# Two-layer hybrid block on one core: large SBUF tiles moved to multiples of 1024 bytes, and VectorE shuffles for a DRAM round trip in the delta rule

## The chip, the cores and the metric

The kernel runs on one core of a Trainium2 chip. The metric is device time in microseconds (us) of one execution; three executions of the kernel before took 1622.04, 1630.62 and 1631.97 us, so the median is 1630.62 us.

## The reference

Two layers, each a half-step SwiGLU, a mixer, and another half-step SwiGLU, over 256 tokens of width 1024:

```
for l in range(DEPTH):                      # DEPTH = 2
    x = x + 0.5 * swiglu(rms_norm(x, ffn1_norm[l]), ...)
    x = x + hybrid_mixer(rms_norm(x, mix_norm[l]), w_in[l], ...)
    x = x + 0.5 * swiglu(rms_norm(x, ffn2_norm[l]), ...)
```

The mixer projects to 11,536 columns and has three branches: a gated linear recurrence (A), dilated windowed attention with 12 heads (B), and a gated delta rule with 8 heads in chunks of 64 tokens (C). Each branch is projected, gated and summed. For each head and chunk the delta rule solves a unit lower triangular system:

```
a = where(strict, einsum('bhnid,bhnjd->bhnij', kb, kc) * decay, 0)
sol = triangular_solve(a + eye(64), concat([vb, kb * exp(gam)]), lower=True, unit_diagonal=True)
```

## The kernel before

**Main matmuls.** Activations are kept transposed (features on partitions, 256 tokens in the free dimension). Each float32 operand of a projection is split into a rounded part and a remainder, both in the type fp32r: tiles `wh` and `wl` for weights, and two slots `s` of 256 columns (1024 bytes per partition) for activations. Each 128x128 weight block then takes three matmuls (high by high, high by low, low by high). In `stationary` (line 479) the weights are the stationary operand, a slice of 128 columns (512 bytes) of `wh` or `wl`, and a slot is the moving operand (256 columns). In `moving` (line 506), used only for the attention's q, k and v projections, the roles are swapped: a 128-column half of a slot is stationary, and 256 columns of `wh` or `wl` move. The results go to PSUM tiles `big`.

**Weights.** SyncE's queue loads 512 KB groups into one of six `raw` tiles, ScalarE (sometimes VectorE) rounds 1024 columns into `wh`, and VectorE subtracts to get `wl` (`convert`, line 430). 24 matmuls use one such chunk.

**Order.** All instructions are recorded by a planner at build time. It keeps a modelled clock for each engine, adds a cost to it for every instruction (`_cost`, line 327), and runs small tasks (Python generators) between main matmuls when their inputs should be there by those clocks. TensorE executes the recorded order as it stands, so a small matmul that stands too early holds back the main ones behind it. `until` lets the planner's TensorE clock run on, with no main matmul recorded, while the next main matmul's input is not due.

**Delta rule.** `pair` (line 994) handles two heads, eight times in all (four in each layer). It cuts 16x16 diagonal blocks out of the triangular matrix into `A16` (128 partitions x 64 columns). The substitution inside a block needs each row on all 16 partitions of that block. So `A16` is written to DRAM (`rd`, 32 KB) and read back into `RR` with every row repeated on 16 partitions (512 KB), both through SyncE's queue, on which the weight loads are issued too; the planner's task clock is moved on by 5.5 and then 8.5 us. GpSimd then does 15 steps of a multiply and a subtraction each (lines 1136 to 1140). TensorE joins the blocks (the 32x32, 64x64 and 128x128 matmuls into PSUM tiles `sm`), and the result `yc` feeds branch C. Attention (`heads4`) runs alongside and gives `yb` to branch B.

**Places in SBUF.** The pool places tiles one after another. In the built program, before the change, `raw`, `wh`, `wl`, `X`, `zr` and `ssq` start 960 bytes past a multiple of 1024 (the first `raw` at byte 26,560, the first `wh` at 51,136), because `cst` (2070 columns) and `prm` (440 columns) come first. The two small tiles `eps_n` and `half` stand behind `ssq` and happen to fill the 64 bytes that are missing, so `tiny`, `arena` and the slots start at multiples of 1024 (102,400, 106,496 and 163,840). A stationary slice of `wh` or `wl` therefore starts 448 or 960 bytes past a multiple of 1024, and the slot that moves against it at a multiple of 1024. In `moving` it is the other way round: the stationary half slot starts at a multiple of 512, and the moving slice at 960.

Of the kernel before, what the change touches and what calls it, by code (L numbers as in the profile page):

```python
# [10 lines left out]
F32 = mybir.dt.float32  # L11
# [6 lines left out]
P = 128  # L18
L = 2
# [20 lines left out]
KEEP, KEEP2 = 3072, 2048  # L40
ARENA_COLS = 14336
NSLOT = 60
SPARE = 4
SLACK = (800.0, 1500.0, 1500.0, 1500.0, 1500.0, 600.0)
URGENT = 2
# [54 lines left out]
def flat_chunks():  # L100
    return [c for layer in all_jobs() for jobs in layer for job in jobs for c in job[2]]


def group_chunks(chunks):
    groups, cur, cols = [], [], 0
    for c in chunks:
        w = c[3] * c[5]
        if cur and cols + w > GROUP_COLS:
            groups.append((cur, cols))
            cur, cols = [], 0  # L110
        cur.append(c)
        cols += w
    groups.append((cur, cols))
    return groups
# [60 lines left out]
class Arena:  # L175
    def __init__(self, pr, ap, unit):
        self.pr, self.ap, self.unit = pr, ap, unit
        self.n = ap.shape[1] // unit
        self.busy = [False] * self.n
        self.stamp = [0.0] * self.n  # L180
        self.peak = 0
# [123 lines left out]
def _free(ap):  # L305
    n = 1
    for x in ap.shape[1:]:
        n *= x
    return n


class Engine:
# [16 lines left out]
    def _cost(self, name, a, k):  # L329
        key = self._key  # L330
        if key == "pe":
            lhsT = k["lhsT"] if name == "matmul" else a[1]
            rhs = k["rhs"] if name == "matmul" else a[2]
            n, m = _free(rhs), _free(lhsT)
            if lhsT.dtype == F32R:
                return max(0.46 * n, 0.83 * m)
            if name == "transpose":
                return 0.84 * max(n, m)
            if m <= 32 and lhsT.shape[0] <= 32:
                return 40.0  # L340
            if m <= 64 and lhsT.shape[0] <= 64 and n <= 64:
                return 100.0
            return 1.7 * max(n, m)
        n = _free(a[0])
        if name == "tensor_reduce":
            n = _free(a[1])
        if key == "a":
            c = 93 + 0.833 * n
            for x in ("scale", "bias", "accum_out"):
                c += 93 * (not isinstance(k.get(x, 0.0), float) and x in k)  # L350
            func = a[2] if name == "activation" else None
            sets = TABLES.get(func)
            if sets and self._pr.table not in sets:
                self._pr.table = sets[0]
                c += 1283
            return c
        if key == "g":
            return (330 + 160 * n) if k.get("op") == ALU.pow else 350 + 0.6 * n
        if name == "reciprocal":
            return 68 + 6.3 * n  # L360
        fast = name in ("tensor_copy", "tensor_scalar") and a[1].space != PSUM
        c = 68 + (0.52 if fast else 1.04) * n
        if name in ("scalar_tensor_tensor", "tensor_scalar") and not isinstance(a[2], float):
            c += 60
        if k.get("accum_out") is not None:
            c += 60
        return c
# [5 lines left out]
class Prog:  # L373
    def __init__(self, ctx, tc, io):
        self.tc, self.nc, self.io = tc, tc.nc, io
        nc = self.nc
        self.clock = {"pe": 0.0, "v": 0.0, "a": 0.0, "g": 0.0}
        self.table = None
        self.cur = self.main = Task(None, 0.0, 0)
        self.step, self.used = set(), {}  # L380
        self.tasks = []
        self.pe, self.v = Engine(self, "pe", nc.tensor), Engine(self, "v", nc.vector)
        self.a, self.g = Engine(self, "a", nc.scalar), Engine(self, "g", nc.gpsimd)
        sb = ctx.enter_context(tc.tile_pool(name="sb", bufs=1))
        ps = ctx.enter_context(tc.tile_pool(name="ps", bufs=1, space=PSUM))
        dr = ctx.enter_context(tc.tile_pool(name="dr", bufs=1, space=bass.MemoryType.DRAM))
        self.cst = sb.tile([P, CST["_n"]], F32, name="cst")
        self.prm = sb.tile([P, L * PRM["_n"]], F32, name="prm")
        self.raw = [sb.tile([P, GROUP_COLS], F32, name=f"raw{i}") for i in range(NRAW)]
        self.wh = [sb.tile([P, 1024], F32R, name=f"wh{i}") for i in range(NCONV)]  # L390
        self.wl = [sb.tile([P, 1024], F32R, name=f"wl{i}") for i in range(NCONV)]
        self.X = sb.tile([P, KD, T], F32, name="X")
        self.zr = sb.tile([P, T], F32, name="zr")
        self.ssq = sb.tile([P, T], F32, name="ssq")
        self.eps_n = sb.tile([P, 1], F32, name="eps_n")
        self.half = sb.tile([P, 8], F32, name="half")
        self.tiny_t = sb.tile([P, 1024], F32, name="tiny")
        self.ar_t = sb.tile([P, ARENA_COLS], F32, name="arena")
        self.tiny = Arena(self, self.tiny_t, 8)
        self.slots = Slots(self, sb, NSLOT)  # L400
        self.ar = Arena(self, self.ar_t, 64)
        self.big = Banks(self, [ps.tile([P, 512], F32, name=f"big{i}") for i in range(NBIG)])
        self.sm = Banks(self, [ps.tile([P, 512], F32, name=f"sm{i}") for i in range(8 - NBIG)])
        self.gdram = [dr.tile([16, P], F32, name=f"gd{l}") for l in range(L)]
        self.rdram = [[dr.tile([P, 64], F32, name=f"rd{l}_{i}") for i in range(4)] for l in range(L)]
        self.rc = [self.tiny.get(16).ap for _ in range(L)]
        self.ea = [self.tiny.get(8) for _ in range(L)]
        self.qg = [self.tiny.get(6) for _ in range(L)]
        self.groups = group_chunks(flat_chunks())
        self.chunk_at = []  # L410
        off = 0
        self.goff = []
        for gi, (cs, cols) in enumerate(self.groups):
            self.goff.append(off)
            c0 = 0
            for c in cs:
                self.chunk_at.append((c, gi, c0, c[3] * c[5]))
                c0 += c[3] * c[5]
            off += P * cols
        self.unread = [len(cs) for cs, _ in self.groups]  # L420
        self.cursor = 0
        self.dma_next = 0
        self.dma_clock = 0.0
        self.raw_t = {}
        self.conv_t = {}
        self.conv_next = 0
        self.when = {}
        self.ops = {}
        self.prepared = set()
        self.nsq = None  # L430
        self.npair = 4
# [111 lines left out]
    def get(self, cols):  # L543
        b = None
        if cols == T:
            b = self.slots.get(F32, SPARE)
        return b or self.ar.get(cols, self.keep())
# [480 lines left out]
    def pair(self, l, h0):  # L1028
# [6 lines left out]
        src = self.gdram[l].rearrange("(t h) i -> h t i", t=2)  # L1035
# [30 lines left out]
        ssk, ssq, c, cn, rb = self.tinies(5, 4)  # L1066
        bt = self.beta.v("p (t h) -> p h t", t=2)[:, h0:h0 + 2, :]
        c4 = lambda x: x.v("p (h t) -> p h t", h=2)
        for hh, h in enumerate(heads):
# [8 lines left out]
            n = 2 * hh  # L1078
# [36 lines left out]
        t1, A16, RR = yield from self.spaces([128, 64, 1024])  # L1115
# [4 lines left out]
        a16 = A16.v("p (n j) -> p n j", n=4)  # L1120
        self.v.tensor_tensor(a16, t4[:, :, 0, :], t4[:, :, 1, :], op=ALU.add)
        yield
        self.nc.sync.dma_start(self.rdram[l][h0 // 2], A16.ap)
        self.cur.t += 5500.0
        yield
        src = self.rdram[l][h0 // 2].rearrange("(b k) c -> b (k c)", k=16)
        self.nc.sync.dma_start(RR.ap, src.unsqueeze(1).to_broadcast([8, 16, 1024]))
        t1.free()
        A16.free()
        self.cur.t += 8500.0  # L1130
        yield
        r4 = RR.v("p (k n j) -> p n k j", n=4, k=16)
        M16, tmp = yield from self.spaces([64, 64])
        m16 = M16.v("p (n j) -> p n j", n=4)
# [21 lines left out]
        b = yield from self.bank()  # L1156
# [9 lines left out]
        b = yield from self.bank()  # L1166
# [13 lines left out]
        b = yield from self.bank()  # L1180
# [19 lines left out]
        b = yield from self.bank()  # L1200
# [16 lines left out]
        b = yield from self.bank()  # L1217
# [9 lines left out]
        b = yield from self.bank()  # L1227
# [27 lines left out]
        b = yield from self.bank()  # L1255
# [7 lines left out]
        b = yield from self.bank()  # L1263
# [8 lines left out]
        for hh in range(2):  # L1272
            n = 2 * hh + 1
# [3 lines left out]
        b = yield from self.bank()  # L1277
# [38 lines left out]
        b = yield from self.bank()  # L1316
# [388 lines left out]
```

## Time and profile before

| what | value |
|---|---|
| median of three executions | 1630.62 us (1622.04 to 1631.97) |
| profiled execution | 1627.63 us, span 1625.4 us |
| mean granted TensorE clock | 0.994 |
| busy in the span: TensorE | 1602.4 us (99%) |
| VectorE, ScalarE, GpSimd | 1159.2 (71%), 936.7 (58%), 139.3 us (9%) |
| DMA queue of the loads, share of 16 engines | 53.7% |

TensorE is called busy wherever a matmul is in flight. One main matmul is in flight for about 280 ns and the next starts some 115 ns after it, so a share of 99% doesn't tell how fast they follow each other: that is read from the distance between starts. The layers run from about 6 to 822 us and from 822 to 1622 us; the first SwiGLU of a layer takes some 190 us, the mixer 435, the second SwiGLU 187.

### The profile page before, as it was taken

To read this page: it belongs to the slowest core of one execution; us is meant where nothing else is said; L and a number is where in the kernel's file an instruction comes from. 1 tells how busy PE (TensorE), PEld (TensorE's weight loads), DVE (VectorE), ACT (ScalarE), POOL (GpSimd) and SP (SyncE) were. 2 spreads that over 40 slices of the span, in tenths; PEclk is the share of its full clock that TensorE was granted. 3 is DMA by queue.
4 is the path that set the end of the run, shared out by engine and by line. 5 is a ranking of instruction groups with operands and counts; after the bars stand their busy time and mean duration, and the time that the engine had idled before them with its cause. 6 is when DMAs were issued, how large, how long until landed. Compare 5 with 4: busy or idle time off the path is not lost. (4 is left out here: it accounts for less than half of the span.)

```text
span 1625.4 us, 34428 instructions
## 1 busy us (share of the span) xinstructions
PE 1602.4 (99%) x13952; PEld 1560.0 (96%) x13952; DVE 1159.2 (71%) x2172; ACT 936.7 (58%) x1643; POOL 139.3 (9%) x280
## 2 busy tenths in 40 slices
PE   9999999999999999999999999999999999999999
PEld 8999999989988999999999999999898899999999
DVE  8666588987973667666566656989878756676653
ACT  7544456878854546444454445568887555554442
POOL 0000000345002000000000000003540120000000
PEclk9999999999998999999999999999999999999999
DMA  8655656544343565555555555656443345655562
GB/s 304 186 187 179 193 179 194 164 162 133 120 129 107 163 204 184 187 188 178 188 192 183 182 185 185 195 176 182 139 140 122 123 131 189 190 184 185 181 188 86
DMA packets 84942, 279.04 MB, mean 172 GB/s; under 512 B 10256, under 2 KB 15664, under 8 KB 84784
## 3 DMA queue, kind: packets, MB, share of 16 engines
q1 hardware_dynamic: 84784, 276.85, 53.7%
q8 instruction: 109, 1.79, 0.4%
q14 instruction: 49, 0.40, 0.1%
HBM read 275.49 MB, written 1.33 MB: 170 GB/s over the span
## 5 line engine op out<-in xcount | busy, mean ns | idle before, releaser
L323 PE MATMUL big<-s,wh 128*128 128x256 f32 (+1 forms) x7520 | 1346.3, 281 | 7.0 <-DVE s L323 6.0
L323 PEld LDWEIGHTS big<-s,wh 128*128 128x128 f32 (+1 forms) x7520 | 1151.0, 188 | 17.4 <-DVE s L323 6.8
L323 PE MATMUL big<-s,wl 128*128 128x256 f32 (+1 forms) x3760 | 1053.6, 280 | 0.0
L323 DVE TENSOR_TENSOR wl<-raw,wh 128x1024 fp32r<-128x1024 f32 (+3 forms) x523 | 620.8, 1187 | 248.4 <-ACT wh L323 245.2
L323 ACT ACTIVATE wh<-raw 128x1024 fp32r<-128x1024 f32 (+4 forms) x497 | 509.1, 1025 | 361.8 <-PE big L323 168.8
L323 PEld LDWEIGHTS big<-s,wl 128*128 128x128 f32 (+1 forms) x3760 | 705.3, 188 | 2.8 <-issue 1.8
L323 ACT ACTIVATE s<-s 128x256 fp32r<-128x256 f32 (+1 forms) x213 | 85.2, 413 | 116.6 <-DVE s L323 116.0
L323 POOL TENSOR_TENSOR tiny<-tiny,half 128x4 f32<-128x4 f32 (+1 forms) x28 | 38.6, 1378 | 1102.0 <-DVE tiny L323 1083.9
L323 PE MATMUL sm<-arena 128*128 128x128 f32 (+7 forms) x1440 | 114.0, 238 | 9.7 <-DVE arena L323 6.9
L323 PEld LDWEIGHTS sm<-arena 32*32 32x32 f32 (+5 forms) x1440 | 85.8, 138 | 30.2 <-issue 9.3
L323 PE MATMUL big<-wh,s 128*128 128x256 f32 x576 | 110.2, 287 | 0.0
L323 POOL TENSOR_TENSOR arena<-arena 128x60 f32<-128x60 f32 (+14 forms) x240 | 98.6, 411 | 62.6 <-DMA arena<-rd 44.7
L323 DVE TENSOR_TENSOR s<-s,s 128x256 fp32r<-128x256 f32 (+1 forms) x181 | 75.7, 422 | 36.5 <-ACT s L323 36.1
L323 PEld LDWEIGHTS big<-wh,s 128*128 128x128 f32 x576 | 89.6, 189 | 1.2
L323 DVE SCALAR_TENSOR_TENSOR s<-big,prm,s 128x255 f32<-128x255 f32 (+2 forms) x183 | 85.6, 477 | 6.6 <-ACT s L323 5.3
L323 DVE TENSOR_TENSOR arena<-big,zr 128x512 f32<-128x512 f32 x88 | 60.9, 692 | 34.8 <-PE big L323 34.5
L323 PE MATMUL big<-wl,s 128*128 128x256 f32 x288 | 82.1, 285 | 0.0
L323 ACT ACT_TABLE_LOAD x63 | 80.8, 1283 | 1.7 <-PEq L1697 0.7
L323 ACT ACTIVATE arena<-sm 128x128 f32<-128x128 f32 (+6 forms) x152 | 48.8, 323 | 37.6 <-PE sm L323 35.1
L323 ACT ACTIVATE s<-big 128x256 f32<-128x256 f32 x53 | 20.2, 382 | 62.1 <-PE big L323 62.1
L323 PEld LDWEIGHTS big<-wl,s 128*128 128x128 f32 x288 | 54.5, 189 | 0.4
L323 ACT ACTIVATE s<-big,prm 128x256 f32<-128x256 f32 x53 | 26.5, 499 | 45.2 <-PE big L323 45.0
(110 smaller groups left out, 772.3 us busy)
## 6 DMA issues: line engine op xcount, KB each, us to landing
raw<-wts SPq DMA_DIRECT2D x435, 512.0 KB, 3.7
raw<-wts SPq DMA_DIRECT2D x64, 448.0 KB, 3.6
raw<-wts SPq DMA_DIRECT2D x16, 384.0 KB, 3.1
arena<-rd SPq DMA_DIRECT2D x8, 512.0 KB
arena<-rgw SPq DMA_DIRECT2D x4, 512.0 KB, 5.2
arena<-gd SPq DMA_DIRECT2D x16, 128.0 KB, 4.7
X<-x SPq DMA_DIRECT2D x4, 256.0 KB, 4.9
raw<-wts SPq DMA_DIRECT2D x4, 256.0 KB, 3.2
```

The source lines that it names most:

```text
L323: r = f(*a, **k)
```

## The change

Three edits. The tiles `eps_n` and `half` move ahead of `raw`, and an unused tile of 252 columns follows them. In the built program `raw`, `wh`, `wl`, `X`, `zr` and `ssq` now start at multiples of 1024 bytes (the first `raw` at 27,648, the first `wh` at 52,224), and `tiny`, `arena` and the slots still do (103,424, 107,520, 164,864). The planner's cost of a main matmul goes from 0.46 to 0.445 ns a column (from 117.8 to 113.9 ns for 256 columns). In `pair`, the write to `rd` and the read back into `RR` are replaced by 15 VectorE shuffles: the shuffle for row k copies, inside each group of 32 partitions, partition 16*(c//16)+k to partition c, for 64 columns, into columns 64k to 64k+63 of `RR`.

```diff
+PAD = 252
...
-                return max(0.46 * n, 0.83 * m)
+                return max(0.445 * n, 0.83 * m)
...
+        self.eps_n = sb.tile([P, 1], F32, name="eps_n")
+        self.half = sb.tile([P, 8], F32, name="half")
+        sb.tile([P, PAD], F32, name="pad")
         self.raw = [sb.tile([P, GROUP_COLS], F32, name=f"raw{i}") for i in range(NRAW)]
...
-        self.eps_n = sb.tile([P, 1], F32, name="eps_n")
-        self.half = sb.tile([P, 8], F32, name="half")
...
-        self.rdram = [[dr.tile([P, 64], F32, name=f"rd{l}_{i}") for i in range(4)] for l in range(L)]
...
-        self.nc.sync.dma_start(self.rdram[l][h0 // 2], A16.ap)
-        self.cur.t += 5500.0
-        yield
-        src = self.rdram[l][h0 // 2].rearrange("(b k) c -> b (k c)", k=16)
-        self.nc.sync.dma_start(RR.ap, src.unsqueeze(1).to_broadcast([8, 16, 1024]))
         t1.free()
+        for k in range(1, 16):
+            self.v.stream_shuffle(RR[:, k * 64:k * 64 + 64], A16.ap, [16 * (c // 16) + k for c in range(32)])
+            if k % 5 == 0:
+                yield
         A16.free()
-        self.cur.t += 8500.0
-        yield
```

Since costs and tasks change, the planner records another order. On VectorE, in the first layer's mixer where the first pair cuts out `A16` (the row `arena<-arena 128x64`), the change has the shuffles in groups of five between the convolutions (`s<-big,prm,s`) and the weights' subtractions (`wl<-raw,wh`):

```order
L324 TENSOR_TENSOR arena<-arena,cst 128x128
L324 SCALAR_TENSOR_TENSOR s_3526<-big_91,prm,s_3526 128x253
L324 TENSOR_TENSOR arena<-arena 128x64
L324 SCALAR_TENSOR_TENSOR s_3563<-big_92,prm,s_3563 128x255
L324 STREAM_SHUFFLE arena<-arena 128x64 x5
L324 TENSOR_TENSOR s_3345<-s_3345,s_2725 128x256
L324 SCALAR_TENSOR_TENSOR s_3563<-big_92,prm,s_3563 128x254
L324 TENSOR_TENSOR wl_83<-raw_75,wh_78 128x1024
L324 SCALAR_TENSOR_TENSOR s_3563<-big_92,prm,s_3563 128x253
L324 STREAM_SHUFFLE arena<-arena 128x64 x5
L324 CAST wh_79<-raw_70 128x1024
...
L324 STREAM_SHUFFLE arena<-arena 128x64 x5
```

All fifteen stand within nine rows of VectorE's order. On SyncE's queue the same place before had the two transfers among the weight loads (`raw<-wts`); the second waits there until the first has landed:

```order
L598 DMA raw_69<-wts 128x1024
L1123 DMA rd_0_100<-arena 128x64
L598 DMA raw_70<-wts 128x1024
L1127 DMA arena<-rd_0_100 128x1x1024
L598 DMA raw_71<-wts 128x1024
```

In the change only weight loads stand there, and the sixteen rows of `rd` are gone from SyncE's order. On TensorE, the first matmuls of branch B's projection in the first layer (tile `big_91`) are followed before by the longest row of small matmuls in the program, 92 of them with no main matmul between; these are its first and last rows, and the main matmul that follows (`s_6190` is branch B's input):

```order
L323 MATMUL big_91<-s_5700,wl_80 128x256
L323 MATMUL sm_93<-arena 128x128
L323 MATMUL sm_93<-arena 128x256
L323 MATMUL sm_96<-arena 128x128
L323 MATMUL sm_96<-arena 128x256
L323 MATMUL sm_95<-arena 32x16 x16
...
L323 MATMUL sm_93<-cst,arena 128x128
L323 MATMUL sm_96<-cst,s_5193 128x128
L323 MATMUL big_91<-s_6190,wh_75 128x256
```

In the change no row of small matmuls in the first layer is longer than 21; the longest is now at the same place of the second layer, with 54:

```order
L324 MATMUL big_91<-s_14986,wl_82 128x256
L324 MATMUL sm_96<-arena 32x32 x12
L324 MATMUL sm_97<-arena 64x64 x4
L324 MATMUL sm_94<-s_15444,s_15406 64x64 x4
...
L324 MATMUL sm_96<-arena 128x128 x2
L324 MATMUL sm_94<-arena 128x128 x2
L324 MATMUL big_91<-s_15495,wh_77 128x256
```

So the place where the planner ran out of main matmuls moved from the first layer to the second and became shorter. In all, 167 groups of small matmuls stand among the main ones before, and 165 in the change.

## Rows read from the trace of the kernel before

**Rows 1.** The page: the span, and each engine's busy time, share of the span and instructions.

```profile
span 1625.4 us, 34428 instructions
PE 1602.4 (99%) x13952; PEld 1560.0 (96%) x13952; DVE 1159.2 (71%) x2172; ACT 936.7 (58%) x1643; POOL 139.3 (9%) x280
```

**Rows 2.** The page's costliest groups, those of the main matmuls: how many, busy time, mean ns of one, and idle time before them. `s,wh` is a slot moving against weights, `wh,s` weights moving against half a slot.

```profile
L323 PE MATMUL big<-s,wh 128*128 128x256 f32 (+1 forms) x7520 | 1346.3, 281 | 7.0 <-DVE s L323 6.0
L323 PE MATMUL big<-s,wl 128*128 128x256 f32 (+1 forms) x3760 | 1053.6, 280 | 0.0
L323 PE MATMUL big<-wh,s 128*128 128x256 f32 x576 | 110.2, 287 | 0.0
L323 PE MATMUL big<-wl,s 128*128 128x256 f32 x288 | 82.1, 285 | 0.0
```

**Rows 3.** TensorE's busy time and number of matmuls in four windows of 50 us in which only main matmuls run, the granted clock, the DMA engines' share and GB/s.

```profile
50.00:100.00 50.00, 50.00 (x427) 1.00 0.61 188
560.00:610.00 50.00, 50.00 (x444) 1.00 0.61 198
700.00:750.00 50.00, 50.00 (x427) 1.00 0.56 179
1360.00:1410.00 50.00, 50.00 (x427) 1.00 0.62 191
```

**Rows 4.** TensorE's timeline where the first projection of the form `moving` begins: start, length of the group, and how many matmuls are in it.

```profile
324.87 0.28 PE L323 MATMUL big<-wh,s 128*128 128x256 f32 x1
324.99 0.28 PE L323 MATMUL big<-wl,s 128*128 128x256 f32 x1
...
325.33 0.28 PE L323 MATMUL big<-wl,s 128*128 128x256 f32 x1
...
326.35 0.28 PE L323 MATMUL big<-wl,s 128*128 128x256 f32 x1
```

**Rows 5.** The same view inside two longer pieces of the form `moving`: 24 matmuls from the first row to the second, 39 from the third to the fourth.

```profile
358.11 0.28 PE L323 MATMUL big<-wl,s 128*128 128x256 f32 x1
...
360.93 0.28 PE L323 MATMUL big<-wl,s 128*128 128x256 f32 x1
...
395.32 0.28 PE L323 MATMUL big<-wl,s 128*128 128x256 f32 x1
...
399.74 0.28 PE L323 MATMUL big<-wl,s 128*128 128x256 f32 x1
```

**Rows 6.** The same view of the form `stationary` around four small transposes.

```profile
539.01 0.28 PE L323 MATMUL big<-s,wl 128*128 128x256 f32 x1
...
539.71 0.28 PE L323 MATMUL big<-s,wl 128*128 128x256 f32 x1
...
539.95 0.60 PE L323 MATMUL sm<-cst,arena 128*128 128x128 f32 x4
...
540.51 0.28 PE L323 MATMUL big<-s,wl 128*128 128x256 f32 x1
...
541.19 0.28 PE L323 MATMUL big<-s,wl 128*128 128x256 f32 x1
```

**Rows 7.** TensorE's busy time, number of matmuls and granted clock in the stretch of the 92 small matmuls (the windows' columns as in rows 3).

```profile
505.00:510.00 5.00, 3.92 (x47) 1.00 0.57 191
510.00:515.00 5.00, 2.93 (x84) 0.55 0.26 79
515.00:520.00 5.00, 4.82 (x45) 0.50 0.01 3
520.00:525.00 5.00, 5.00 (x29) 0.59 0.00 0
```

**Rows 8.** Groups of VectorE instructions, by shape: how many, busy time, mean ns of one, and idle time before them.

```profile
L323 DVE STREAM_TRANSPOSE arena<-arena 128x128 f32<-128x128 f32 x16 | 4.9, 306 | 0.2
L323 DVE TENSOR_TENSOR tiny<-tiny 128x8 f32<-128x8 f32 x28 | 4.6, 169 | 0.5 <-POOL tiny L323 0.4
L323 DVE TENSOR_TENSOR wl<-raw,wh 128x1024 fp32r<-128x1024 f32 x433 | 529.9, 1224 | 196.5 <-ACT wh L323 193.4
```

**Rows 9.** Busy time (and instructions) of PE, PEld, DVE, ACT and POOL in a stretch of a SwiGLU and in those parts of both mixers where the delta rule is prepared, then the granted clock, DMA share and GB/s.

```profile
50.00:100.00 50.00, 50.00 (x427) 50.00 (x427) 34.78 (x45) 23.96 (x36) 0.00 (x0) 1.00 0.61 188
198.00:325.00 127.00, 126.83 (x1040) 123.76 (x1039) 111.90 (x258) 88.33 (x142) 12.71 (x31) 1.00 0.56 180
325.00:405.00 80.00, 76.62 (x867) 71.85 (x866) 65.00 (x186) 63.21 (x157) 41.53 (x74) 0.98 0.47 150
405.00:440.00 35.00, 33.78 (x294) 31.30 (x294) 32.88 (x76) 29.34 (x67) 1.29 (x1) 1.00 0.29 92
1009.00:1133.00 124.00, 123.83 (x1014) 120.97 (x1014) 110.11 (x255) 86.65 (x141) 15.09 (x33) 1.00 0.59 182
```

**Rows 10.** SyncE's timeline at the first pair's round trip: start, length, the write to `rd` and the read back.

```profile
298.31 0.39 SPq L1123 DMA_DIRECT2D rd<-arena  x1
...
302.11 0.70 SPq L1127 DMA_DIRECT2D arena<-rd  x1
```

**Rows 11.** GpSimd's timeline at the same pair: its first run of substitution steps, with the idle time ahead and what ended it.

```profile
311.50 10.82 POOL L323 TENSOR_TENSOR arena<-arena 128x60 f32<-128x60 f32 x24 [13.14 <-DMA arena<-rd]
```

**Rows 12.** The page's form view of GpSimd: the first substitution step of all eight pairs (two instructions each), mean ns of one, and the idle time ahead of them.

```profile
L323 POOL TENSOR_TENSOR arena<-arena 128x60 f32<-128x60 f32 x16 | 6.8, 425 | 45.6 <-DMA arena<-rd 44.7
```

## The prediction

> **What bounds the kernel now.** I read the page's busy times first: TensorE is busy for 1602.4 of 1625.4 us, VectorE for 71% of the span, the others less [rows 1]. So all waits of TensorE together are 23 us, and a change that takes more than that must make TensorE's own work shorter. The work is 7520 + 3760 + 576 + 288 = 12,144 main matmuls [rows 2], each in flight for about 281 ns. That is not what one costs. They overlap, and the cost is the distance from one start to the next.
>
> For that I went to windows in which nothing but main matmuls runs. 50 us hold 427 of them in three windows and 444 in the fourth, all at a granted clock of 1.00, the upper level of 2.4 GHz [rows 3]. A window also counts the matmuls in flight at its edge, 2.4 on average (281 ns over some 118). So the distance is 50/424.6 = 117.8 ns in three windows and 50/441.6 = 113.2 ns in the fourth. TensorE has two paces at the same clock. Load doesn't separate them: the DMA share is 0.61 in a slow window and 0.61 in the fast one.
>
> The timeline shows where it changes pace. At the first projection of the form `moving` two matmuls start 0.12 us apart, and from 325.33 to 326.35 nine take 1.02 us, 113.3 ns each [rows 4]. The pace then holds: 24 matmuls in 2.82 us (117.5 ns) in one piece, 39 in 4.42 us (113.3 ns) in another [rows 5]. In the form `stationary`, six starts take 0.70 us before four small transposes and 0.68 us after them [rows 6], and the fast pace stays until 635 us. I went through all starts of main matmuls that follow each other. 10,479 distances are slow (116 to 123 ns, mean 117.8) and 1285 fast (112 to 115, mean 113.4); the rest are waits. By form the shares differ: in `moving` 419 of 742 are fast, in `stationary` 866 of 11,022, and 820 of these lie in the one stretch from 540 to 635 us.
>
> What differs between the forms is where operands start. In `moving` the stationary operand (half a slot) starts at a multiple of 512 bytes and the moving one 64 bytes below a multiple of 1024; in `stationary` it is the stationary one that is 64 below. I read this as: a stationary operand on a multiple of 512 lets TensorE fall into the fast pace, 1 to 4 matmuls after an interruption, while one that is 64 bytes off nearly always holds it in the slow one. It isn't the whole story. The stretch from 540 us is fast with the operand 64 off, and one piece in [rows 5] is slow with it aligned. The pace has two self-holding states, and the address shifts the odds.
>
> **Edit 1, the places.** After it all main matmuls have a stationary operand on a multiple of 512 and a moving one on a multiple of 1024. This pair of offsets does not occur among the main matmuls of before, so the trace can't show it. Bounds: no gain, or all 10,479 slow distances at 113.4, 10,479 x 4.4 ns = 46.1 us. I choose within by stage. The SwiGLUs and the tail of the second mixer hold 7038 slow distances (from 15 to 198, 635 to 1009 and 1345 to 1622 us) with hardly an interruption; I take all as fast, 7038 x 4.4 = 31.0 us. The other 3441 lie between the groups of small matmuls. After each of these some slow ones come first, so I take the share of `moving`, 56%: 3441 x 0.56 x 4.4 = 8.5 us. Sum 39.5 us. The faster pace asks for a chunk of weights every 2.7 us instead of 2.8. In the SwiGLU VectorE is busy 34.8 of 50 us, ScalarE 24.0 and the DMA engines 0.61 [rows 9], so all go up by 4% of that, and none becomes the bound.
>
> Against this stands a rule. The Trainium skill, page "SBUF — State Buffer", section "Who interferes with whom", says that TensorE and ScalarE never wait on anyone for SBUF, and the page "TensorE: Matmul & The Clock Gate", section "Back-to-back issue gap", gives N/2.4 + 2.5 ns with no address in it, an estimate of 109.2 ns for 256 columns. By these pages this edit would do nothing. The trace fits neither fully, since it has two paces, both above that estimate; the first rival below is the case in which addresses don't count.
>
> **Edit 2, the planner's cost.** 113.9 ns instead of 117.8 costs nothing itself. It moves small matmuls by as much as main ones get faster, if edit 1 works; if not, the planner's clock runs 3% ahead of TensorE, so other engines have more time, not less.
>
> **Edit 3, shuffles for the round trip.** 8 x 15 = 120 shuffles of 64 columns. The trace has none. The nearest rows are the transpose of 128 columns at 306 ns and an operation on 8 columns at 169 [rows 8]. On the line between them 64 columns are 169 + 137 x 56/120 = 233 ns (bounds 169 and 306). That is 28.0 us on VectorE (20.3 to 36.7), 14 in each mixer, 3.5 for a pair. It takes the place of 13.2 us from the write's issue at 298.31 to the first substitution step at 311.50 [rows 10, 11]. But of this GpSimd alone knew: its waits for the read back sum to 44.7 us [rows 12], and TensorE was filled with main matmuls meanwhile, so the shorter chain is worth nothing by itself. What hides the 14 us is VectorE's idle time: from 198 to 405 us it is busy 111.9 + 65.0 of 207, so 30 us are free, and 13.9 from 1009 to 1133 alone [rows 9]. A group of five (1.2 us) stands ahead of weight subtractions of 1.22 us each [rows 8]; five chunks are in the ring, so TensorE has up to four chunks, 10.9 us, before it misses one. I take 1 us lost, from 0 to the full 28 if that cover is gone, as from 405 to 440, where VectorE is busy 32.9 of 35 [rows 9]. Sixteen transfers fewer on SyncE's queue: TensorE doesn't wait for loads, so 0.
>
> **The order.** The row of 92 small matmuls cost TensorE idle time of 1.1 + 2.1 + 0.2 us from 505 to 520, and its busy time there ran at half clock: 2.93 x 0.45 + 4.82 x 0.50 + 5.00 x 0.41 = 5.8 us [rows 7]. Together 9.1 us. It goes, and a row of 54 comes in the second layer; in proportion that costs 54/92 x 9.1 = 5.3, so 3.8 us are won (0 to 9.1).
>
> **Sum**, against the profiled execution of 1627.6 us (3.0 below the median of 1630.6): 1627.6 - 39.5 + 1.0 - 3.8 = 1585.3, so 1585 us, 2.8% under the median. The uncertainty of the small terms, about 10 us either way, gives this case 1575 to 1597.
>
> **Rivals.** *The pace stays a draw:* every stretch keeps the pace into which it happened to fall, with the odds of `moving` throughout. 10,479 x 0.56 x 4.4 = 25.8, so 1627.6 - 25.8 + 1.0 - 3.8 = 1599 us, with long stretches at 117.8. For it speaks the slow piece in [rows 5]; against it, that a SwiGLU is one long piece with many chances to fall over. *Addresses don't count* (or it was the moving operand's 64 bytes that helped, and these are now lost): 1627.6 + 1.0 - 3.8 = 1625 us. For it speaks the fast stretch with unaligned weights [rows 6]; against it, 56% beside 8%. *A third, faster pace:* the four transposes take 0.60 us, so they start (0.60 - 0.28)/3 = 107 ns apart [rows 6]; at 107 all main matmuls would save 10,479 x 10.8 + 1285 x 6.4 = 121 us, which gives 1503. Nothing shows it for main matmuls. *Slower:* the shuffles delay the weight subtractions in the mixers and TensorE stands. With all 28 us on the path and the pace unchanged, 1627.6 + 28.0 - 3.8 = 1652. It decides once VectorE has under 14 us free where a mixer's shuffles stand, and only if the pace stays, since the SwiGLUs alone win 31.
>
> **How the numbers follow.** Forecast 0.60, draw 0.18, addresses don't count 0.13, third pace 0.04, slower 0.05. The range from 1562 to 1612 holds the first two, 0.78, with the bounds of their small terms. About 1% is what a measurement of this kernel can tell from no change (16 us): the forecast, the draw and the third pace are faster by more, 0.82; the second rival is within, 0.13; the last slower, 0.05.
>
> **What would show it.** Windows of 50 us in the SwiGLUs should hold 443 or 444 matmuls, not 427; if one holds 427 it was the draw, if all do, addresses don't count. A shuffle should take about 0.23 us, and TensorE's waits for `wl` should stay near nothing in the mixers. TensorE's idle time should be near 20 us, and a stretch at half clock may show in the second mixer. The forecast is wrong if the SwiGLUs keep 117.8 ns, or if TensorE's idle time grows by more than 10 us.

## The result, and the profile after

The change makes the kernel slower, by 1.3%. Four executions took 1649.57 to 1654.67 us, median 1651.82 us, against 1631.3 us (1622.04 to 1632.39, four executions) of the kernel before: a ratio of 1.0128, 95% interval [1.0105, 1.0152]. The prediction was 1585 us, and its range ended at 1612. The profiled execution took 1649.57 us, 21.9 us more than that of before.

The page after, the lines that answer to [rows 1, 2]: the span, each engine's busy time, and the four groups of main matmuls (count, busy time, mean ns in flight, idle time before).

```profile
span 1647.4 us, 34626 instructions
PE 1629.2 (99%) x13952; PEld 1587.6 (96%) x13952; DVE 1166.5 (71%) x2395; ACT 933.1 (57%) x1658; POOL 141.7 (9%) x280
...
L324 PE MATMUL big<-s,wh 128*128 128x256 f32 (+1 forms) x7520 | 1372.7, 284 | 6.3 <-DVE s L324 2.8
...
L324 PE MATMUL big<-s,wl 128*128 128x256 f32 (+1 forms) x3760 | 1067.7, 284 | 0.1
...
L324 PE MATMUL big<-wh,s 128*128 128x256 f32 x576 | 112.2, 289 | 0.0
...
L324 PE MATMUL big<-wl,s 128*128 128x256 f32 x288 | 83.2, 289 | 0.0
```

The counts are the same, and TensorE is again idle for only 18 us. What grew is its own work: busy time by 26.8 us, and a main matmul of each group is in flight 2 to 4 ns longer. The four windows of [rows 3], read after the change (TensorE's busy time and matmuls, granted clock, DMA share, GB/s), show what that means:

```profile
50.00:100.00 50.00, 50.00 (x419) 1.00 0.58 188
560.00:610.00 50.00, 50.00 (x419) 1.00 0.59 189
700.00:750.00 50.00, 50.00 (x419) 1.00 0.57 181
1360.00:1410.00 50.00, 50.00 (x419) 1.00 0.62 192
```

Before, such a window held 427 or 444 matmuls; now all four hold 419, at the same granted clock of 1.00. With the 2.4 in flight at the edge, 50/416.6 = 120.0 ns from one start to the next. This pace doesn't occur as a lasting one before. TensorE's timeline shows it in both forms; first 24 matmuls of `stationary`, then 24 of `moving`, from the first row of each piece to its last:

```profile
699.80 0.28 PE L324 MATMUL big<-s,wl 128*128 128x256 f32 x1
...
702.68 0.28 PE L324 MATMUL big<-s,wl 128*128 128x256 f32 x1
```

```profile
346.07 0.28 PE L324 MATMUL big<-wl,s 128*128 128x256 f32 x1
...
348.94 0.28 PE L324 MATMUL big<-wl,s 128*128 128x256 f32 x1
```

They take 2.88 and 2.87 us: 120.0 and 119.6 ns, as near as rows with two decimals allow. Over all starts, 11,693 distances lie between 116 and 123 ns with a mean of 119.9, and 56 between 112 and 115. The draw between two paces is gone, and what took its place is slower than both.

That is the whole loss. Before, the mean over both kinds was (10,479 x 117.8 + 1285 x 113.4)/11,764 = 117.3 ns; now it is 119.87. Over 11,750 distances the difference is 30.1 us. The rest went down by 8.2 us: the distances with a small matmul at one end or both from 185.7 to 178.8 us in all, and what the other distances between main matmuls take beyond the pace by 1.3. Together that is the +21.9 us.

Next the shuffles. The form view of VectorE, and its timeline at the first and last shuffles of the first pair:

```profile
L324 DVE STREAM_SHUFFLE arena<-arena 128x64 f32<-128x64 f32 x120 | 18.8, 223 | 0.0
...
L324 DVE LOAD_MASK_SELECT arena<-arena x120 | 1.6, 13 | 0.0
```

```profile
311.29 0.23 DVE L324 STREAM_SHUFFLE arena<-arena 128x64 f32<-128x64 f32 x1
...
311.43 0.22 DVE L324 STREAM_SHUFFLE arena<-arena 128x64 f32<-128x64 f32 x1
...
316.49 0.23 DVE L324 STREAM_SHUFFLE arena<-arena 128x64 f32<-128x64 f32 x1
```

One takes 223 ns, but the next starts after 0.14 us: their ends overlap, as those of matmuls do. With the load of its selector it adds (18.8 + 1.6)/120 = 0.17 us of busy time. The fifteen of the first pair are spread over 5.4 us, with subtractions and convolutions between, and GpSimd's steps begin right behind them, where [rows 11] showed a wait for the read back:

```profile
316.85 15.52 POOL L324 TENSOR_TENSOR arena<-arena 128x60 f32<-128x60 f32 x30 [5.52 <-DVE arena L324]
```

Over all eight pairs GpSimd's wait ahead of its first step is 26.9 us, where [rows 12] had 44.7. It buys nothing that TensorE waited for. The shuffles also take nothing. Among the waits of TensorE's matmuls there is none for `wl`, and the largest sums are (us in all, times, longest)

```profile
PE big L324 <- DVE s L324: 2.8, 5, 0.8
PE sm L324 <- ACT arena L324: 2.3, 2, 1.7
PE sm L324 <- DVE arena L324: 2.3, 3, 1.1
```

Its weight loads (PEld) read `wl` too, and wait for it 0.6 us in the whole program, where they waited 0.5 us before:

```profile
PEld big L324 <- DVE wl L324: 0.4, 2, 0.3
PEld sm L324 <- DVE wl L324: 0.2, 1, 0.2
```

The row of 54 small matmuls in the second layer left its mark where the order said, and a shorter stretch at half clock stands in the first layer (columns of the windows as above):

```profile
1330.00:1335.00 5.00, 2.80 (x56) 1.00 0.31 97
1335.00:1340.00 5.00, 4.41 (x21) 0.56 0.01 3
1340.00:1345.00 5.00, 4.92 (x30) 0.76 0.00 0
450.00:455.00 5.00, 4.05 (x21) 1.00 0.72 252
455.00:460.00 5.00, 5.00 (x31) 0.66 0.36 108
```

### The profile page after: what moved, and what is told of

Same layout as the page of the kernel before. It is cut to its first block, busy times and chain, and to the rows that moved or that the text cites. A ratio compares the mean times of both kernels' runs of the same rounds, so it can differ in the third digit from the quotient of the medians.

```text
span 1647.4 us, 34626 instructions
## 1 busy us (share of the span) xinstructions
PE 1629.2 (99%) x13952; PEld 1587.6 (96%) x13952; DVE 1166.5 (71%) x2395; ACT 933.1 (57%) x1658; POOL 141.7 (9%) x280
## 5 line engine op out<-in xcount | busy, mean ns | idle before, releaser
L324 PE MATMUL big<-s,wh 128*128 128x256 f32 (+1 forms) x7520 | 1372.7, 284 | 6.3 <-DVE s L324 2.8
L324 PEld LDWEIGHTS big<-s,wh 128*128 128x128 f32 (+1 forms) x7520 | 1175.0, 192 | 15.9 <-issue 6.2
L324 PE MATMUL big<-s,wl 128*128 128x256 f32 (+1 forms) x3760 | 1067.7, 284 | 0.1
L324 ACT ACTIVATE wh<-raw 128x1024 fp32r<-128x1024 f32 (+3 forms) x493 | 506.0, 1027 | 469.0 <-issue 259.8
L324 PEld LDWEIGHTS big<-s,wl 128*128 128x128 f32 (+1 forms) x3760 | 720.8, 192 | 4.0 <-issue 3.1
L324 POOL TENSOR_TENSOR tiny<-tiny,half 128x4 f32<-128x4 f32 (+1 forms) x28 | 43.2, 1545 | 1123.8 <-DVE tiny L324 1089.8
L324 PE MATMUL sm<-arena 128*128 128x128 f32 (+8 forms) x1444 | 113.0, 235 | 3.5 <-ACT arena L324 2.3
L324 POOL TENSOR_TENSOR arena<-arena 128x60 f32<-128x60 f32 (+14 forms) x240 | 95.0, 396 | 44.9 <-DVE arena L324 26.9
L324 DVE SCALAR_TENSOR_TENSOR s<-big,prm,s 128x255 f32<-128x255 f32 (+1 forms) x177 | 83.4, 477 | 14.0 <-ACT s L324 12.6
```

What stands on the lines that cost most here:

```text
L324: r = f(*a, **k)
```

## The experiments

All are compared with the kernel before, run in turns with it on the same chip. In each of them TensorE, VectorE, ScalarE and GpSimd run the same instructions in the same order as the kernel that it is made from, before or the change. Letters in the expectations stand for the theories that they spell out. "Difference" is the start of the weights' tiles `wh` and `wl` minus the start of a slot, in bytes: 960 before, 0 after.

**Which edit?** The first kernel has edit 1 alone, the second edits 2 and 3 with the places of before.

```diff
+PAD = 252
...
+        self.eps_n = sb.tile([P, 1], F32, name="eps_n")
+        self.half = sb.tile([P, 8], F32, name="half")
+        sb.tile([P, PAD], F32, name="pad")
         self.raw = [sb.tile([P, GROUP_COLS], F32, name=f"raw{i}") for i in range(NRAW)]
...
-        self.eps_n = sb.tile([P, 1], F32, name="eps_n")
-        self.half = sb.tile([P, 8], F32, name="half")
```

> The kernel before with edit 1 alone (the large tiles on multiples of 1024, planner's cost and round trip as before). Theory A, the places alone made the change slower: the main matmuls start 120 ns apart as in the changed kernel, so 10,479 slow distances grow by 2.2 ns and 1285 fast ones by 6.6 ns, 31.5 us in all, and the time is about 1659 us (1652 to 1664). Theory B, the new order and the shuffles made it slower: the pace stays at 117.8 ns and the time at 1622 to 1634 us.

Measured: 1653.91 us, ratio 1.0144 [1.013, 1.0158], with 11,693 distances of mean 119.9 ns and 63 of 113.3, as Theory A has it. The loss is all in edit 1.

The second is the changed kernel with edit 1 taken back:

```diff
-PAD = 252
...
-        self.eps_n = sb.tile([P, 1], F32, name="eps_n")
-        self.half = sb.tile([P, 8], F32, name="half")
-        sb.tile([P, PAD], F32, name="pad")
...
+        self.eps_n = sb.tile([P, 1], F32, name="eps_n")
+        self.half = sb.tile([P, 8], F32, name="half")
```

> The changed kernel with the places of before (edits 2 and 3 alone). Theory A: the pace is 117.8 ns again, and what is left of the difference is what the two traces show outside the pace, 8 us in favour of the change: 1615 to 1627 us. Theory B: the pace is 120 ns in spite of the places of before, or VectorE holds TensorE back, and the time is about 1650 us.

Measured: 1628.45 us, ratio 0.9991 [0.9981, 1.0], no difference to speak of. The pace is that of Theory A and the time 1.5 us above its range: of the 8 us in favour, 1.8 show in the medians. 11,315 distances are near 117.8 ns and 428 near 113.4; before, 1285 were near 113.4, so in the profiled execution the draw took 857 x 4.4 = 3.8 us back.

**Which property of the places?** The places differ in more than one way: absolute starts, the difference of the two operands, and its sign. The next kernels are the kernel before, with its order, and only the tiles moved. For the first, all large tiles start 64 bytes past a multiple of 1024 and the slots stay on one, so the difference is 64:

```diff
+PAD = 16
...
+        self.eps_n = sb.tile([P, 1], F32, name="eps_n")
+        self.half = sb.tile([P, 8], F32, name="half")
+        sb.tile([P, PAD], F32, name="pad")
...
-        self.eps_n = sb.tile([P, 1], F32, name="eps_n")
-        self.half = sb.tile([P, 8], F32, name="half")
+        sb.tile([P, 240], F32, name="gap")
         self.tiny_t = ...
```

> The kernel before with weights, raw tiles and X starting 64 bytes past a multiple of 1024 (before: 960), slots and arena still on multiples of 1024. Theory A1, the pace hangs on the difference of the two operands' starts (moving minus stationary, modulo 512; 0 gives 120 ns, +64 gives 117.8, -64 gives 113.4): stationary-form matmuls now have -64, so their distance falls to 113.4 and the moving-form ones rise to 117.8: about 1583 us (1576 to 1595). Theory A2, each operand's own start counts (a moving operand on a multiple of 1024 is what is slow, a stationary one off 512 as before): 117.8 ns or more, 1622 to 1640 us.

Measured: 1604.48 us (1595.69 to 1613.2), ratio 0.9833 [0.9791, 0.9875], faster than before and than the change. It lies outside both ranges: by Theory A2 nothing was to be faster than before, and by Theory A1 all of `stationary` should be fast, where 5532 of its 11,009 distances are; before, 866 of 11,022 were. Of the four windows, all in `stationary`, two hold 439 or 440 matmuls; that at 560 us was fast before too [rows 3], that at 1360 was not:

```profile
50.00:100.00 50.00, 50.00 (x427) 1.00 0.57 187
560.00:610.00 50.00, 49.81 (x439) 1.00 0.57 201
700.00:750.00 50.00, 50.00 (x427) 1.00 0.54 183
1360.00:1410.00 50.00, 49.81 (x440) 1.00 0.61 199
```

The timeline at 206 us shows the pace fall over. Up to here it was 117.8 ns since 15 us; two small matmuls come between, and from 207.08 to 208.78 fifteen distances take 1.70 us, 113.3 ns each:

```profile
206.25 0.31 PE L324 MATMUL sm<-cst,s 40*128 40x40 f32 x2
...
207.08 0.28 PE L324 MATMUL big<-s,wl 128*128 128x256 f32 x1
...
208.78 0.28 PE L324 MATMUL big<-s,wl 128*128 128x256 f32 x1
```

The second of this kind has all tiles, the slots too, 960 bytes past a multiple of 1024 (the pad is 240 columns, and no gap), so that no operand is aligned and the difference is 0:

> The kernel before with every large tile, the slots and the arena too, 960 bytes past a multiple of 1024. Theory A1 (difference of starts, here 0): 120 ns, about 1659 us, as on multiples of 1024. Theory A2 (own starts): not 120 ns, since no main operand starts on a multiple of 512; 113 to 118 ns, 1580 to 1632 us.

Measured: 1654.14 us (one execution), 11,663 distances of mean 119.9, and the windows of the change:

```profile
50.00:100.00 50.00, 50.00 (x419) 1.00 0.57 182
1360.00:1410.00 50.00, 50.00 (x419) 1.00 0.55 182
```

So it is the difference that counts and not where the operands stand. The arena moved with the slots in every kernel, so a difference of the weights to the arena would fit these times as well. But the two forms use the same tiles in one kernel, and their paces differ, with the roles of the operands swapped: before, 419 of 742 distances in `moving` are fast and 8% in `stationary`.

**What is its period?** The same edit with other sizes: a pad of 32, 64, 96 and 8 columns with gaps of 224, 192, 160 and 248, for differences of 128, 256, 384 and 32.

> The kernel before with weights, raw tiles and X 128 bytes past a multiple of 1024, slots and arena on multiples (two operands' starts differ by 128). Theory N, nearness: the closer the two starts are to each other (modulo 512) the worse; 64 bytes gave a draw between 113.3 and 117.8 ns, so 128 gives the fast pace throughout: 10,479 x 4.4 = 46 us won, 1580 to 1588 us. Theory E, equality alone matters: every difference but 0 gives the draw, 1595 to 1632 us. Theory S, sign: only a negative difference helps, and more of it doesn't: 1595 to 1613 us.

Measured: 1640.02 us, ratio 1.0054 [1.0032, 1.0076], slower than before. None of the three theories had that.

> As the run with 128 bytes, with 256: the farthest that two starts can be apart modulo 512. Theory N: the fast pace throughout or a still faster one, 1580 to 1588 us or less. Theory E: the draw, 1595 to 1632 us.

Measured: 1653.17 us, ratio 1.0129 [1.01, 1.0159], 11,695 distances of 119.9. A difference of 256 is as bad as 0, which neither theory had. Its windows are those of the change:

```profile
50.00:100.00 50.00, 50.00 (x419) 1.00 0.55 182
560.00:610.00 50.00, 50.00 (x419) 1.00 0.57 196
```

> As before, with 384 bytes, which is 128 on the other side modulo 512 (before stands 64 on that side, where slow distances were 89%). Theory N: like the run with 128 bytes, 1580 to 1590 us. Theory S: the slow pace of before, about 1630 us. Theory E: the draw, 1595 to 1632 us.

Measured: 1641.87 us, ratio 1.0057 [1.0035, 1.008]: the time of 128, and outside all three ranges. With 256 as 0 and 384 as 128, a period of 256 bytes took the place of the theories above.

> As before, with 32 bytes. Theory N: worse than 64 bytes, between the draw there (1604 us) and the 120 ns of equal starts (1654 us): 1610 to 1654 us. Theory E: the draw as at 64 bytes, 1595 to 1613 us.

Measured: 1635.77 us, ratio 1.0035 [1.0021, 1.0049], in the range of Theory N, which 128 and 256 had ruled out. No two sharp paces here: distances spread from 115 to 123 ns.

**Does the period hold, and is it the matmul's operands alone?** Four kernels tried what follows from it. A difference of 320 (pad 80, gap 176) should act as 64, whatever the order of the numbers:

> Kernel before with large tiles 320 bytes past a multiple of 1024 (64 modulo 256), slots on multiples of 1024. If the period is 256 bytes: the paces of e3_plus64, 117.8 and 113.3 ns with about half fast, 1595 to 1615 us. If the period of 256 holds only for the worst case: something else, 1625 or more, with a pace not seen in e3.

Measured: 1598.79 us (two executions), ratio 0.9811 [0.9787, 0.9835], with 3965 distances of 117.8 and 7794 of 113.3. It does: windows hold 427 and 444 matmuls again.

```profile
50.00:100.00 50.00, 50.00 (x427) 1.00 0.57 187
700.00:750.00 50.00, 50.00 (x444) 1.00 0.56 187
```

A difference of 96 (pad 24, gap 232):

> Kernel before with large tiles 96 bytes past a multiple of 1024, slots on multiples of 1024. If the pace depends smoothly on the distance from a multiple of 64 within 256 bytes: between +64 and +128, mean 116 to 119 ns, 1605 to 1640 us. If odd multiples of 32 are a class of their own, as +32 suggests: mean about 118.2 with few at 113.4, 1632 to 1638 us.

Measured: 1634.26 us, ratio 1.0035 [1.0022, 1.0048], the time of 32; distances again spread, from 115 to 122. Both ranges hold it, so this run doesn't tell the two ideas apart.

In edit 1 the places of `raw`, `X`, `zr` and `ssq` changed as well, which DMA, ScalarE and VectorE read and write. This kernel moves them as the change does, and leaves `wh` and `wl` 960 past a multiple of 1024:

```diff
+        sb.tile([P, PAD], F32, name="pad")
         self.raw = ...
+        sb.tile([P, 240], F32, name="gap")
         self.wh = ...
+        sb.tile([P, 16], F32, name="gap2")
         self.X = ...
```

> Kernel before with raw, X, zr and ssq on multiples of 1024, but wh and wl left 960 past one. If only the starts of the two matmul operands count (M): pace 117.8 with some 4 to 11 per cent of fast distances, 1622 to 1632 us, within 0.4% of before. If it was the reads of raw or X by DMA, ScalarE and VectorE that collide with TensorE's (rival): pace 119.9, 1650 to 1655.

Measured: 1628.66 us, ratio 0.9991 [0.9979, 1.0004], 10,493 distances of 117.8 and 1258 of 113.4, as before. But the fast stretch is in another place. Before, the window at 560 held 444 and that at 1360 held 427 [rows 3]; here it is the other way round:

```profile
560.00:610.00 50.00, 50.00 (x427) 1.00 0.58 195
700.00:750.00 50.00, 50.00 (x427) 1.00 0.56 183
1360.00:1410.00 50.00, 50.00 (x444) 1.00 0.62 202
```

So which stretch gets the fast pace is not fixed by the program's order, and the tiles that only other engines touch don't matter.

**The version that beats both.** The changed kernel, with a pad of 16 columns in place of 252 and a gap of 240 ahead of `tiny`:

> The changed kernel with one thing altered: large tiles start 64 bytes past a multiple of 1024 instead of on it; slots stay on multiples of 1024, so the difference of the two operands' starts in `stationary` is 64 modulo 256. If only that difference sets the pace (M): two paces, 117.8 and 113.3 ns, with some 4000 to 7000 fast distances, as in e3_plus64; time 1604 with about -3 from edits 2 and 3, so 1595 to 1612 us. If the changed order or the shuffles bring something that the pace hid (rival): below 1590. If starting near a multiple of 1024 in itself is what cost: above 1640.

Measured: 1596.07 us (1590.73 to 1611.64), ratio 0.9813 [0.9777, 0.9849]. 8689 distances are fast, more than the 4000 to 7000 expected, and 3028 slow; all four windows are at the fast pace or near it:

```profile
50.00:100.00 50.00, 50.00 (x444) 1.00 0.59 198
560.00:610.00 50.00, 49.81 (x439) 1.00 0.57 193
700.00:750.00 50.00, 50.00 (x444) 1.00 0.58 186
1360.00:1410.00 50.00, 49.81 (x440) 1.00 0.59 193
```

All kernels together, by their difference modulo 256. The counts and means are those of one profiled execution each, over both forms. The difference is that of `stationary`, with some 11,000 of the distances counted; the 618 to 742 in `moving` have it with the sign turned, 256 less the number given:

| difference mod 256 | kernel (difference) | 116 to 123 ns: count, mean | 112 to 115 ns: count, mean | time, us |
|---|---|---|---|---|
| 0 | after (0) | 11,693, 119.9 | 56, 113.4 | 1651.82 |
| 0 | places alone (0) | 11,693, 119.9 | 63, 113.3 | 1653.91 |
| 0 | all tiles at 960 (0) | 11,663, 119.9 | 60, 113.3 | 1654.14 |
| 0 | 256 | 11,695, 119.9 | 64, 113.3 | 1653.17 |
| 32 | 32 | 10,929, 118.4 | 771, 114.8 | 1635.77 |
| 64 | 64 | 6050, 117.8 | 5691, 113.3 | 1604.48 |
| 64 | 320 | 3965, 117.8 | 7794, 113.3 | 1598.79 |
| 64 | change with 64 | 3028, 117.8 | 8689, 113.3 | 1596.07 |
| 96 | 96 | 10,168, 118.3 | 1479, 115.0 | 1634.26 |
| 128 | 128 | 9503, 119.6 | 2243, 114.9 | 1640.02 |
| 128 | 384 | 9788, 119.6 | 1951, 114.9 | 1641.87 |
| 192 | before (960) | 10,479, 117.8 | 1285, 113.4 | 1629.87 to 1631.45 |
| 192 | shuffles alone (960) | 11,315, 117.8 | 428, 113.4 | 1628.45 |
| 192 | raw and X alone (960) | 10,493, 117.8 | 1258, 113.4 | 1628.66 |

## Why the prediction was wrong

**What bounds the kernel** held. TensorE's own pace decides, waits are small, and all that moved the time by more than a few us in twelve kernels was the distance between starts.

**The two paces and their link to addresses** were read rightly from the trace, and a step further was taken that the trace didn't carry. The failed step is the sentence "I read this as: a stationary operand on a multiple of 512 lets TensorE fall into the fast pace". Two forms had been seen, which differ in two things at once: which operand is aligned, and the sign of the difference between them. The prediction chose alignment. It is the difference, stationary minus moving, modulo 256: 64 in `moving` and 192 in `stationary`, with more than half and 8% of the distances fast. The kernel of the difference 64 swapped the forms and the shares went with the sign: in it `stationary` is fast for 5532 of 11,009, and `moving`, now at 192, for 158 of some 730. With all tiles at 960 nothing was aligned and the time was that of the change, and at 256 the pace was that of 0.

**The bounds of edit 1** failed with it: "no gain, or all 10,479 slow distances at 113.4". The prediction said that this pair of offsets does not occur among the main matmuls of before, and still took the slow pace as the worst that could come. The new pair had a pace of its own, 120.0 ns, and the term that was put at -39.5 us measured +30.1. A pair that wasn't seen can lie on either side of those that were; had the bound gone as far below nothing as above, the same 4.4 ns on the other side (+46 us), the range would have reached the result.

**The rivals.** The draw and the case "addresses don't count" both kept 117.8 ns as the slow end, so neither ended where the time did. The second stood by the Trainium skill, page "TensorE: Matmul & The Clock Gate", section "Back-to-back issue gap", which has no address in its distance; the formula that the prediction took from it is the page's for one matmul by itself. The runs with the order of before and other places, from 1598.79 to 1654.14 us, don't agree with that. The rival named as *slower* forecast 1652 us, 0.2 us from the result, by a mechanism that did not happen: waits for `wl` are 0.6 us in all. That its time came near is luck. Two slips of the prediction change nothing: 1585.3 us with 10 us either way ends at 1595, not 1597, and the case in which addresses don't count is its second rival, not its first.

**Edit 3, the shuffles:** 233 ns each was near the 223 ns that one takes, but as a price it was too high, since the next one starts 0.14 us later. The sum is 20.4 us of VectorE with the selectors instead of 28.0. That they would be hidden was right: TensorE's idle time did not grow (23 us before, 18 after), and shuffles with the new order alone measured 0.9991. So was the other half: a shorter wait of GpSimd is worth nothing.

**The order** was to give 3.8 us. By the working of the prediction, the row of 54 costs 2.2 + 0.6 + 0.1 us idle and 4.41 x 0.44 + 4.92 x 0.24 = 3.1 us at half clock, 6.0 instead of the 5.3 forecast, and the shorter stretch from 450 to 460 another 1.0 + 1.7; together 8.7. Before, it was 9.1 for the long row and another 0.02 x 76.6 = 1.5 us at a lower clock from 325 to 405 [rows 9]. So by these rows the order gave about 2 us. The medians agree as far as they go, and neither difference is clear of the spread: edits 2 and 3 show 2.1 us between the places alone and the change, and 1.8 between before and the shuffles alone, in whose profiled execution 3.8 us of draw stand against them. Of the 8.2 us that all but the pace gave back in the profiled execution, 6.5 also appear with the places alone, in the order of before. About half of these are the clock: before, the granted clock was lower around 12 and 367 us, and in the execution with the places alone it was not (two rows of before, then two of the places alone):

```profile
10.00:20.00 10.00, 9.16 (x60) 0.83 1.03 416
360.00:380.00 20.00, 17.75 (x217) 0.91 0.52 160
10.00:20.00 10.00, 9.09 (x68) 1.00 1.03 415
360.00:380.00 20.00, 18.38 (x235) 1.00 0.40 134
```

By the working above that is 9.16 x 0.17 + 17.75 x 0.09 = 3.2 us. Whether the rest goes with the slower pace or varies from run to run stays open.

**What stays open.** The runs show how the pace hangs on the difference, not which unit collides with what: the load of the next stationary operand overlaps the running matmul (weight loads are in flight for 96% of the span and matmuls for 99%), and whether it is its read, against that of the moving operand, was not separated. Nor is it known what picks one of the two paces at 64 and 192 when a stretch begins. Four executions of the kernel of the difference 64 took 1595.69 to 1613.2 us, those of the change 1649.57 to 1654.67; so the draw seems to fall out anew in each execution, though only one of each has a trace. At 64, 5691 to 8689 of the distances were fast, and 3028 to 6050 still are not; a way to force it, worth up to 6050 x 4.5 = 27 us in the kernel of the difference 64, was not found.

## What to carry to other kernels

Where matmuls follow each other without a wait, read the distance between starts, and try the difference of the two operands' places as a knob of its own: here 64 bytes instead of 0 in that difference moved the time from 1654 to 1604 us in the same order of instructions, and the difference of 0, which aligning all tiles brings, was with 256 the worst of those tried. When two cases in a trace differ in two things, the trace can't say which one counts; price a third, unseen combination on both sides of those that were seen. A share of 99% busy hides a change of 2 to 6% in the pace.

## What the runs showed of the hardware

The distance between the starts of two 128x256 matmuls with a weight load each, both operands fp32r, at a granted clock of 1.00, goes by the stationary operand's start minus the moving one's, modulo 256 bytes: 120.0 ns at 0, a spread of 115 to 123 ns at 32, 96 and 128 (at 128 a sixth to a fifth of the distances at 115, the others with a mean of 119.6), and two paces that hold themselves, 117.8 and 113.3 ns, at 64 and 192 (in the kernel of the difference 64 one ran for 1578 distances in a row, the other for 1574). In `stationary`, 50 to 78% of the distances were at the faster of them in three kernels at 64, and 0.3 to 8% in three at 192; in `moving`, 53 to 56% at 64 and 19 to 22% at 192. A shuffle of 128x64 float32 values takes 223 ns and starts every 0.14 us with its selector's load.
